# Normalized tokens of an attention phase written to DRAM by pairs of tiles, with the first pair's writes placed behind the third tile's loads

## The chip, the cores and the metric

One core of a Trainium2 chip runs the whole program. The metric is device time in microseconds (us), the median over several executions. The engines: PE is TensorE (matrix products), DVE is VectorE, ACT is ScalarE, POOL is GpSimd, and SP is SyncE, which computes nothing here and issues every DMA, one after the other, in program order. Each engine works through its own instruction list in order; an instruction that waits on a semaphore holds all that stand behind it on that engine.

## What is computed

One step of a one-layer hybrid encoder for 2048 prompt tokens and 32 sample tokens, D = 1024:

```python
n = rmsnorm(x, g_mix); z = n @ w_in            # q, k, v | GLA q, k, v | gate r | low-rank c
a = sink_attend(q, k, v, sinks, window of 128) # softmax per head, chunks of 64
g = rmsnorm(gla_chunked(qg, kg, vg, log_a)) * silu(r)
h = x + concat(a, g) @ w_out
y = h + relu(rmsnorm(h) @ w_up)**2 @ w_down
```

Outputs are y for prompt and sample tokens, the last 128 rows of k and v, and the GLA state. All is float32; a product is made of three passes of high and low parts (h and l).

## The kernel before

Tokens are worked on in 16 tiles of 128 (0 to 15) and one sample tile of 32 (named nt). There are three phases: attention, gated linear attention (GLA), feed-forward. The change lies in the attention phase and in the place where the GLA phase reads back what attention wrote.

**Per tile in the attention phase.** `front(t)` loads the transposed tokens `xT1a` (L249), scales them on DVE (L267), rounds them to a high part `nT..h` on ACT (L270) and takes the low part `nT..l` on POOL (L271). One pair of buffers (h and l) holds two tiles, an even one and the odd one after it; the pool of such buffers has 4, that is 2 pairs. `scales(t)` loads the tokens again untransposed as `x1a` (L244) and makes the row scale `rstd` by a square on ACT (L189) and a small iteration on DVE. `store(t)` writes three things to DRAM for the GLA phase: `rs` (L285: 128 rows of 4 bytes, one per partition), and the tile's halves of `nTh` and `nTl` (L287: 512 KB each). Then come the projections `zq`, `zkv`, `zr` on PE (all at L111), and `attend(t)`: transposes `qTp` and `kTp`, the copies `qT` (DVE, L456), `caT` (DVE, L395) and `kW` (ACT, L466), the scores `S`, a softmax (DVE L499 and L500, ACT L505), transposes `pT` and products `O`. The gate goes to DRAM as `rgd` (L375).

**The order.** The loop at L555 works on the front of the next tile while PE is at the current one. Tiles 0 and 1 are projected together first; the third tile, tile 2, is loaded in the loop's second step. `tc.issue_after(x)` keeps the DMAs in its block behind instruction x on SP. Otherwise a list scheduler with a timeline of its own sets each engine's order when the kernel is built. Weight loads go through five `io` buffers (`stage`, `x1a`, `xT1a`, `rg` and others share them), so a load waits until its buffer has been read.

**DMA semaphores.** SP's DMAs use eight semaphores in turn (DMAHW0 to DMAHW7). A DMA waits until the one eight places before it has landed.

**Reading back.** `gla_tokens(h, tiles)` (L620) loads the tokens of a pair of tiles into a buffer `nTb` (L627, one DMA per tile and part) and each tile's row scale, broadcast, into `rb` (L628).

Of the kernel before, what the change touches and what calls it, by code (L numbers as in the profile page):

```python
# [9 lines left out]
F32 = mybir.dt.float32  # L10
# [9 lines left out]
P = 128  # L20
D = 1024
KB = D // P
NT = 16
NS = 32
# [4 lines left out]
class Builder:  # L29
    def __init__(self, ctx, tc, a, o, nt=NT, ffn=True):  # L30
        self.ctx, self.tc, self.nc, self.a, self.o = ctx, tc, tc.nc, a, o
        self.nt, self.with_ffn = nt, ffn
        nc = self.nc
        self.V, self.S, self.G, self.T, self.Q = nc.vector, nc.scalar, nc.gpsimd, nc.tensor, nc.sync
        pool = lambda name, bufs, **kw: ctx.enter_context(tc.tile_pool(name=name, bufs=bufs, **kw))
        self.const = pool("const", 1)
        self.small = pool("small", 3)
        self.io = pool("io", 5)
        self.w = pool("w", 8)
        self.dram = pool("dram", 1, space=DRAM)  # L40
        self.psm = pool("psm", 3, space=PSUM)
        self.pss = pool("pss", 5, space=PSUM)
        tiles = list(range(nt)) + [nt]
        dt = lambda shape, name: self.dram.tile(shape, F32, tag=name, name=name)
        self.mixT = [dt([P, KB, self.rows(t)], f"mixT{t}") for t in tiles]
        self.nTd = [[dt([P, KB, self.rows(t)], f"nT{x}{t}") for x in "hl"] for t in tiles]
        self.cad = [dt([16, self.rows(t)], f"ca{t}") for t in tiles]
        self.rsd = [dt([self.rows(t), 1], f"rs{t}") for t in tiles]
        self.rgd = [dt([self.rows(t), 512], f"rgd{t}") for t in tiles]

        self.last_pe = self.last_table = None
        self.clock = 0.0
        self.state_clock = -1e9
        self.tasks = []
        self.seq = 0
# [174 lines left out]
    def attention_phase(self):  # L230
        tc, a, V, S, G, Q = self.tc, self.a, self.V, self.S, self.G, self.Q
        nt = self.nt
        w_in = a["w_in"].rearrange("(k p) n -> p k n", p=P)
        with ExitStack() as ctx:
# [4 lines left out]
            nT, st = {}, {}  # L239

            def load_x(t):
                r = self.rows(t)
                x = self.io_tile(f"x1a_{t}")[:r]
                Q.dma_start(x, self.x_src(t))  # L244
                return x

            def load_xT(t):
# [4 lines left out]
            def front(t, xT=None):  # L252

                r = self.rows(t)
                xT = xT or load_xT(t)
                if t == nt:
                    nT[t] = (*(c.tile([P, KB, NS], F32R, tag=f"nTs{x}", name=f"nTs{x}") for x in "hl"), 0)
                elif t % 2 == 0:
                    nT[t] = (*self.tok_pair(f"nT_{t}", 2 * P), 0)
                else:  # L260
                    nT[t] = (*nT[t - 1][:2], P)
                h, l, off = nT[t]
                ts = slice(off, off + r)
                step = 2 if t == 0 else 4
                for k in range(0, KB, step):
                    ks = slice(k, k + step)
                    V.tensor_tensor(  # L267
                        out=xT[:, ks], in0=xT[:, ks], in1=self.gmix[:, ks].unsqueeze(2).broadcast_to([P, step, r]), op=ALU.mult
                    )
                    S.activation(h[:, ks, ts], xT[:, ks], AF.Copy)  # L270
                    (V if t in (0, nt) else G).tensor_tensor(  # L271
                        out=l[:, ks, ts], in0=xT[:, ks], in1=h[:, ks, ts].bitcast(F32), op=ALU.subtract
                    )

            def scales(t, x=None):

                r = self.rows(t)
                x = x or load_x(t)
                V.tensor_copy(self.rstd[:r, t : t + 1], self.rms(x, x, r, f"a{t}"))

            def store(t):

                r = self.rows(t)
                h, l, off = nT[t]
                Q.dma_start(self.rsd[t], self.rstd[:r, t : t + 1])  # L285
                for x, dst in zip((h, l), self.nTd[t]):
                    Q.dma_start(dst, x[:, :, off : off + r].bitcast(F32))  # L287

            order = [*range(10), nt, *range(10, nt)]
            eng = (("act", "pool"), ("dve", "dve"))  # L290
# [35 lines left out]
            def project_q(t):  # L326
                r = self.rows(t)
                rs = self.rstd[:r, t : t + 1]
                qk = wk.tile([P, 5, 2, 64], F32, tag="qk", name=f"qk_{t}", bufs=3)
                sq = self.io_tile(f"sq_{t}")[:, :640].rearrange("p (j v d) -> p j v d", j=5, v=2)  # L330
                ps = self.ps_m(f"zq_{t}")[:r]
                token_gemm(ps, t, wq)
                pv = ps.rearrange("p (v j d) -> p j v d", v=2, j=4)
                S.activation(qk[:r, 0:4], pv, AF.Copy, scale=rs)
                S.activation(sq[:r, 0:4], pv, AF.Square, scale=rs)
                return qk, sq
# [31 lines left out]
            def project_gate(t):  # L368

                r = self.rows(t)  # L370
                rg = self.io_tile(f"rg_{t}")[:r, :512]
                ps = self.ps_m(f"zr_{t}")[:r]
                token_gemm(ps, t, wr)
                V.tensor_scalar(out=rg, in0=ps, scalar1=self.rstd[:r, t : t + 1], scalar2=None, op0=ALU.mult)
                Q.dma_start(self.rgd[t], rg)  # L375
# [180 lines left out]
            for i, t in enumerate(order):  # L556
                for j in order[i + 1 : i + 2 + (nt in order[i + 1 : i + 2])]:
                    if j not in nT:
                        front(j)
                        scales(j)  # L560
                        store(j)
                if i == 0:
                    z = {j: project_q(j) for j in order[:2]}
                    z = {j: project_kv(j, *z[j]) for j in z}
                    with tc.issue_after(self.weights_in):
                        store(t)
                        store(order[1])
                elif i > 1:
                    z[t] = project_kv(t, *project_q(t))
                if t == nt - 1:  # L570
                    self.prepare_gla(0)
                self.spawn(attend_sample(*z.pop(t)) if t == nt else attend(t, *z.pop(t)))
                if t != nt - 2:
                    project_gate(t)
                if t == nt - 1:
                    project_gate(t - 1)
                if t == nt:
                    self.load_gla_consts()
# [39 lines left out]
            self.wvg += self.wide_pairs(w_in, 1280, "wvg", self.GLA_ENG, (1,))  # L618

    def gla_tokens(self, h, tiles):  # L620
        pair = self.tok_pair(f"nTb_{h}", 288)
        rb = self.mid.tile([P, 288], F32, tag="rb", name=f"rb_{h}")
        off = 0
        for t in tiles:
            r = self.rows(t)
            for x, src in zip(pair, self.nTd[t]):
                self.Q.dma_start(x[:, :, off : off + r].bitcast(F32), src)  # L627
            self.Q.dma_start(rb[:, off : off + r], self.rsd[t].rearrange("r o -> o r").broadcast_to([P, r]))  # L628
            off += r
        return pair, off, rb  # L630
# [811 lines left out]
```

## Time and profile before

| | us |
|---|---|
| runs (median of 3, lowest, highest) | 2326.0, 2319.54, 2327.71 |
| the profiled execution | 2323.38 |
| its span, first to last instruction | 2321.6 |
| mean granted clock of TensorE | 0.979 of full speed |

Some 1.8 us of the profiled execution lie outside its span. PE is busy 97% of the span, DVE 61%, POOL 52%, ACT 41%. In the profile, "[7.28 <-ACT nT_2h L270]" behind an instruction says that its engine sat idle for 7.28 us before it and that this ACT instruction ended the wait. Numbers of buffers are left out there, so `nT_2h` stands for the buffer of tiles 2 and 3, and a name without its tile number can be that of any tile.

### The profile page before, as it was taken

How to read it: one execution, taken by the hardware profiler on the slowest of the kernel's cores; microseconds unless marked ns; L12 is line 12 of the kernel's file. 1: busy time of each engine (PE TensorE's matmuls, PEld its weight loads, DVE VectorE, ACT ScalarE, POOL GpSimd, SP SyncE). 2: the span in 40 equal slices, each digit the busy share in tenths (PEclk: the TensorE clock that was granted, in tenths of full speed). 3: DMA queues.
4: the chain of work that ended last, by engine and by line, in shares of the span. 5: the costliest groups of instructions: out<-in, count | busy, mean ns of one | idle time of the engine just before them, and what ended most of it. 6: DMA issues, size and time to landing. Idle time of an engine off the chain costs nothing.

```text
span 2321.6 us, 39805 instructions
## 1 busy us (share of the span) xinstructions
PE 2256.5 (97%) x15389; PEld 2117.4 (91%) x15389; DVE 1410.5 (61%) x3631; ACT 952.7 (41%) x1953; POOL 1197.3 (52%) x995
## 2 busy tenths in 40 slices
PE   6999998899998999999999999999999999999999
PEld 5777776788877999999999999999999999999999
DVE  6666656788888755555553755555554755555555
ACT  3554445455552643333434533333334533333331
POOL 3222224223241387667765566666655386666662
PEclk8999999889999999999999999999999999999999
DMA  8864564232322422222236222222227122222221
GB/s 204 159 130 109 122 149 154 56 95 70 103 84 76 129 76 91 92 74 73 73 103 181 75 81 73 73 73 73 73 63 218 55 73 73 73 73 73 73 64 52
DMA packets 214462, 221.57 MB, mean 95 GB/s; under 512 B 38736, under 2 KB 178976, under 8 KB 214272
## 3 DMA queue, kind: packets, MB, share of 16 engines
q1 hardware_dynamic: 214272, 219.02, 34.0%
q8 instruction: 121, 1.98, 0.4%
q14 instruction: 69, 0.57, 0.1%
HBM read 180.08 MB, written 38.91 MB: 94 GB/s over the span
## 4 chain that ended last, share of the span: by engine, by line
PE 75%; DVE 11%; DMA 5%; POOL 3%; ACT 3%; issue 2%; SPq 1%; DVEq 0%; POOLq 0%; ACTq 0%
PE dn L111 31%; PE PA22T L111 4%; PE PS3T L111 4%; PE PS2T L111 4%; PE PS4B L111 4%; PE PS1T L111 4%; PE PA11B L111 4%; PE PA12B L111 4%; PE zq L111 3%; PE op L111 3%; PE zr L111 3%; DVE AT L889 2%; PE zkv L111 2%; PE zv L111 2%; PE O L111 1%
## 5 line engine op out<-in xcount | busy, mean ns | idle before, releaser
L1100 POOL TENSOR_TENSOR wu<-stage,wu 128x512 fp32r<-128x512 f32 x336 | 432.2, 1297 | 469.2 <-ACT wu L1099 456.0
L1276 DVE TENSOR_TENSOR y<-y,dn 128x360 f32<-128x360 f32 (+1 forms) x768 | 393.1, 515 | 226.9 <-PE dn L111 224.2
L1099 ACT ACTIVATE wu<-stage 128x512 fp32r<-128x512 f32 x336 | 206.1, 628 | 493.7 <-PE dn L111 212.2
L1102 POOL TENSOR_TENSOR stage<-stage 128x512 f32<-128x512 f32 x192 | 249.3, 1298 | 7.5
L1229 ACT ACTIVATE r<-PA11B 128x360 f32<-128x360 f32 (+1 forms) x48 | 22.0, 459 | 283.6 <-PE PA11B L111 283.6
L1214 DVE TENSOR_TENSOR PA12B<-PA12B,r 128x360 f32<-128x360 f32 (+1 forms) x48 | 25.3, 527 | 150.6 <-PE PA12B L111 150.6
L716 POOL TENSOR_TENSOR g<-g,ggla 128x512 f32<-128x512 f32 (+1 forms) x17 | 25.2, 1501 | 170.0 <-ACT g L119 170.0
L111 PE MATMUL PA22T<-T4h,wu 128*128 128x360 f32 (+1 forms) x384 | 101.7, 328 | 0.0
L111 PE MATMUL PS2T<-T2h,wu 128*128 128x360 f32 (+1 forms) x384 | 99.4, 321 | 1.0 <-POOL wu L1100 0.6
L111 PE MATMUL PS3T<-T3h,wu 128*128 128x360 f32 (+1 forms) x384 | 100.2, 324 | 0.1
L111 PE MATMUL PS4B<-B22h,wu 128*128 128x360 f32 (+1 forms) x384 | 99.1, 321 | 0.0
L111 PE MATMUL PS1T<-T1h,wu 128*128 128x360 f32 (+1 forms) x384 | 98.9, 321 | 0.0
L111 PE MATMUL PA11B<-B11h,wu 128*128 128x360 f32 (+1 forms) x384 | 98.8, 321 | 0.0
L111 PE MATMUL PA12B<-B21h,wu 128*128 128x360 f32 (+1 forms) x384 | 98.7, 321 | 0.0
L889 DVE COPY_PREDICATED AT<-masks,A 64x64 f32<-64x64 int32 (+1 forms) x330 | 83.0, 253 | 13.8 <-PE A L111 3.9
L813 POOL TENSOR_TENSOR E<-cc 128x256 f32<-128x256 f32 (+1 forms) x117 | 68.3, 617 | 24.9 <-PE A L111 19.7
L505 ACT ACTIVATE P<-S,negm 128x192 f32<-128x192 f32 (+2 forms) x128 | 51.6, 418 | 53.0 <-DVE negm L500 36.1
L111 PEld LDWEIGHTS PA22T<-T4h,wu 128*128 128x128 f32 x384 | 70.3, 194 | 0.0
L111 PEld LDWEIGHTS PS2T<-T2h,wu 128*128 128x128 f32 x384 | 68.1, 188 | 1.8 <-ACT T2h L1132 1.0
L111 PEld LDWEIGHTS PS3T<-T3h,wu 128*128 128x128 f32 x384 | 69.2, 191 | 0.4 <-ACT T3h L1132 0.4
L111 PEld LDWEIGHTS PS1T<-T1h,wu 128*128 128x128 f32 x384 | 68.1, 188 | 0.0
L111 PEld LDWEIGHTS PS4B<-B22h,wu 128*128 128x128 f32 x384 | 68.1, 188 | 0.0
(1008 smaller groups left out, 7738.8 us busy)
## 6 DMA issues: line engine op xcount, KB each, us to landing
stage<-in_w_up SPq DMA_DIRECT2D x96, 512.0 KB, 3.8
stage<-in_w_down SPq DMA_DIRECT2D x96, 512.0 KB, 3.8
stage<-in_w_out SPq DMA_DIRECT2D x24, 512.0 KB, 4.2
xT1a<-in_xT_prompt SPq DMA_DIRECT2D x16, 512.0 KB, 6.8
stage<-in_w_in SPq DMA_DIRECT2D x16, 512.0 KB, 8.8
x1a<-in_x_prompt SPq DMA_DIRECT2D x16, 512.0 KB, 5.3
out_yT_prompt<-y SPq DMA_DIRECT2D x32, 180.0 KB, 5.2
m<-mixT SPq DMA_DIRECT2D x11, 512.0 KB, 4.1
```

What stands on the lines that cost most here:

```text
L111: self._pe(self.T.matmul(out, lhsT, rhs, start=start, stop=stop), ns)
L505: S.activation(Pt[:, u, :n], sp[:, jp], AF.Exp, bias=negm[:, ch, u : u + 1], scale=0.125, accum_out=rsum[:, ch, u : u + 1],)
L716: G.tensor_tensor(out=gv, in0=gv, in1=ggla[:r].unsqueeze(1).broadcast_to([r, 4, P]), op=ALU.mult)
L813: G.tensor_tensor(out=e4, in0=c4, in1=ref, op=ALU.subtract)
L889: V.copy_predicated(dst, mk.unsqueeze(1).broadcast_to([L // nh, 2, w // m, m]), src[r].rearrange("s p (n m) -> s p n m", m=m),)
L1099: self.after(S.activation(h, src, AF.Copy), after)
L1100: G.tensor_tensor(out=l, in0=src, in1=f32(h), op=ALU.subtract)
L1102: tt = lambda o, x, y, op: G.tensor_tensor(out=o, in0=x, in1=y, op=op)
L1214: tt = lambda out, x, y, op=ALU.add: V.tensor_tensor(out=out, in0=x, in1=y, op=op)
L1229: S.activation(r0, product(b, "A11", "B11"), AF.Copy)
L1276: V.tensor_tensor(out=yg[:, f, :], in0=yg[:, f, :], in1=ps, op=ALU.add)
```

## The change

Three edits. The DRAM buffers `nTd` hold a pair of tiles instead of one. `store(t)` writes `rs` for each tile as before, and `nTh` and `nTl` of both tiles of a pair in one DMA each after the odd tile (the sample tile on its own); `gla_tokens` reads them in the same size, and its buffer is as wide as its tiles need, so that a partition's row of a pair lies in one piece of 8 KB. And the stores of tiles 0 and 1 move from the loop's first step, behind the last weight load, to its second step, behind the load of tile 2's `x1a`.

```diff
-        self.nTd = [[dt([P, KB, self.rows(t)], f"nT{x}{t}") for x in "hl"] for t in tiles]
+        self.nTd = [[dt([P, KB, 2 * P if t < nt else NS], f"nT{x}{t}") for x in "hl"] for t in range(0, nt + 1, 2)]
...
-                Q.dma_start(x, self.x_src(t))
+                self.x_load = Q.dma_start(x, self.x_src(t)).ins
...
-                h, l, off = nT[t]
                 Q.dma_start(self.rsd[t], self.rstd[:r, t : t + 1])
-                for x, dst in zip((h, l), self.nTd[t]):
-                    Q.dma_start(dst, x[:, :, off : off + r].bitcast(F32))
+                if t == nt or t % 2:
+                    for x, dst in zip(nT[t], self.nTd[t // 2]):
+                        Q.dma_start(dst, x.bitcast(F32))
...
+                if i == 1:
+                    with tc.issue_after(self.x_load):
+                        store(0)
+                        store(1)
                 if i == 0:
                     z = {j: project_q(j) for j in order[:2]}
                     z = {j: project_kv(j, *z[j]) for j in z}
-                    with tc.issue_after(self.weights_in):
-                        store(t)
-                        store(order[1])
...
-        pair = self.tok_pair(f"nTb_{h}", 288)
+        pair = self.tok_pair(f"nTb_{h}", sum(self.rows(t) for t in tiles))
...
-            for x, src in zip(pair, self.nTd[t]):
-                self.Q.dma_start(x[:, :, off : off + r].bitcast(F32), src)
+            if t == nt or t % 2 == 0:
+                for x, src in zip(pair, self.nTd[t // 2]):
+                    self.Q.dma_start(x[:, :, off : off + src.shape[2]].bitcast(F32), src)
```

SP's list goes from 594 rows to 562. Line numbers of the changed kernel are one to four higher. The order of PE's instructions is the same in both kernels.

SP, early in the attention phase. Before, the six stores of tiles 0 and 1 (rs, nTh, nTl, twice) stand ahead of the small loads; these are the last rows of them and what follows, up to the load of tile 2's xT1a (`ck` to `masks` are small constants):

```order
L287 DMA nTl_93<-nT_0l 1024x1x128 [waits DMAHW7_49]
L285 DMA rs_144<-rstd 128x1 [waits DMAHW0_49,DVE_49]
L287 DMA nTh_94<-nT_0h 1024x1x128 [waits DMAHW1_49]
L287 DMA nTl_95<-nT_0l 1024x1x128 [waits DMAHW2_49]
L403 DMA ck<-in_cache_k 128x128 [waits DMAHW3_49]
L404 DMA cv<-in_cache_v 128x128 [waits DMAHW4_49]
L602 DMA wal<-in_w_alpha 16x256 [waits DMAHW5_49]
L603 DMA d_2829<-in_resets 128x288 [waits DMAHW6_49]
L604 DMA masks<-in_masks 128x224 [waits DMAHW7_49]
L628 DMA rb_4297<-rs_143 128x128 [waits DMAHW0_49]
L628 DMA rb_4297<-rs_144 128x128 [waits DMAHW1_49]
L249 DMA xT1a_528<-in_xT_prompt 128x1024 [waits DMAHW2_49,DVE_49]
```

The same place on SP in the changed kernel, from tile 2's xT1a (506) to tile 3's (587):

```order
L250 DMA xT1a_506<-in_xT_prompt 128x1024 [waits DMAHW2_49,DVE_49]
L245 DMA x1a_516<-in_x_prompt 128x1024 [waits DMAHW3_49,Pool_49]
L376 DMA rgd_144<-rg_478 128x512 [waits DMAHW4_49,DVE_49]
L285 DMA rs_127<-rstd 128x1 [waits DMAHW5_49]
L285 DMA rs_128<-rstd 128x1 [waits DMAHW6_49]
L288 DMA nTh_92<-nT_0h 128x2048 [waits DMAHW7_49]
L288 DMA nTl_93<-nT_0l 128x2048 [waits DMAHW0_49]
L632 DMA rb_4265<-rs_127 128x128 [waits DMAHW5_49,DMAHW1_49]
L632 DMA rb_4265<-rs_128 128x128 [waits DMAHW6_49,DMAHW2_49]
L250 DMA xT1a_587<-in_xT_prompt 128x1024 [waits DMAHW3_49,Activation_49]
```

Tile 2's load now stands ahead of the stores. The two `rs` stores follow each other, and the two `rb` loads, which wait for them (DMAHW5 and DMAHW6 are theirs), stand ahead of tile 3's load.

ACT at the same place, before, from the rounding of tile 2 (`nT_2h<-xT1a_528`) to the first exponentials; `xT1a_607` is tile 3's, `kW_600` and `kW_675` are the key windows of tiles 0 and 1:

```order
L270 ACTIVATE nT_2h<-xT1a_528 128x4x128 [waits DMAHW2_49,DVE_49]
L270 ACTIVATE nT_2h<-xT1a_528 128x4x128 [waits DVE_49]
L189 ACTIVATE x1a_538,ss_a_540<-x1a_538 128x1024 [waits DMAHW3_49,Pool_49]
L466 ACTIVATE kW_600<-kTp_588 128x128 [waits DVE_49]
L270 ACTIVATE nT_2h<-xT1a_607 128x4x128 [waits DMAHW6_49,DVE_49]
L270 ACTIVATE nT_2h<-xT1a_607 128x4x128 [waits DVE_49]
L466 ACTIVATE kW_675<-kTp_663 128x128 [waits DVE_49]
L505 ACTIVATE P_0_681,rsum_679<-S_0_0_682,negm_678 128x64 [waits DVE_49,PE_49]
```

And in the changed kernel, from the key window of tile 0 (`kW_580`) to that of tile 1 (`kW_655`); `xT1a_587` is tile 3's:

```order
L467 ACTIVATE kW_580<-kTp_568 128x128 [waits DVE_49]
L506 ACTIVATE P_0_661,rsum_659<-S_0_0_662,negm_658 128x64 [waits DVE_49,PE_49]
L506 ACTIVATE P_0_661,rsum_659<-S_0_0_662,negm_658 128x64
L506 ACTIVATE P_0_661,rsum_659<-S_0_1_663,negm_658 128x64 [waits DVE_49,PE_49]
L506 ACTIVATE P_0_661,rsum_659<-S_0_1_663,negm_658 128x64
L382 ACTIVATE es_0_676<-es_0_676 128x4 [waits DVE_49]
L335 ACTIVATE qk_617<-zq_619,rstd 128x512 [waits PE_49]
L336 ACTIVATE sq_618<-zq_619,rstd 128x512 [waits Activation_49]
L271 ACTIVATE nT_2h<-xT1a_587 128x4x128 [waits DMAHW3_49,DVE_49]
L271 ACTIVATE nT_2h<-xT1a_587 128x4x128 [waits DVE_49]
L467 ACTIVATE kW_655<-kTp_643 128x128 [waits DVE_49]
```

In both, the key window of tile 1 stands behind the rounding of tile 3; that rounding has moved behind tile 0's exponentials and tile 2's `qk` and `sq`.

PE, in the changed kernel, where it first needs tile 1's key window, in the middle of tile 2's projections (in the kernel before the rows are the same, with `kW_675`):

```order
L112 MATMUL zkv_691<-wkvh,nT_2h 128x272
L112 MATMUL zkv_691<-wkvl,nT_2h 128x272
L112 MATMUL zkv_691<-wkvh,nT_2l 128x272
L112 MATMUL S_0_0_742<-kW_655,qT_649 128x192 [waits Activation_49,Pool_49]
L112 MATMUL S_0_1_743<-kW_655,qT_649 128x192 [waits DVE_49]
L112 MATMUL S_0_0_742<-kW_655,qT_649 128x192
L112 MATMUL S_0_1_743<-kW_655,qT_649 128x192
```

Nothing has moved on PE; the first S row of tile 1 waits for ACT's `kW_655`.

## Rows read from the trace of the kernel before

**Rows 1.** Who waited longest on PE, whole program: total us, times, longest us.
```profile
PE zq L111 <- ACT nT_2h L270: 7.3, 1, 7.3
...
PE O L111 <- ACT pS L535: 3.5, 2, 3.1
```

**Rows 2.** Three stretches: us, then busy us (and instructions) of PE, its weight loads, DVE, ACT, POOL, then TensorE's granted clock, busy share of the DMA engines, GB/s.
```profile
47.90:55.10 7.20, 0.00 (x0) 0.00 (x0) 1.40 (x3) 0.67 (x2) 0.00 (x0) 0.64 0.86 272
55.10:60.38 5.28, 5.08 (x11) 3.55 (x12) 3.04 (x14) 1.76 (x4) 2.75 (x3) 0.52 0.62 150
60.38:340.00 279.62, 279.45 (x1618) 215.94 (x1617) 182.50 (x703) 142.35 (x464) 70.62 (x118) 1.00 0.63 136
```

**Rows 3.** The chain that ended last, in order of time: start us, us, what.
```profile
31.65 17.41 DMA nTl<-nT_0l
...
49.13 4.54 DMA xT1a<-in_xT_prompt
...
54.43 1.24 ACT nT_2h L270 x2
...
71.89 9.91 DMA xT1a<-in_xT_prompt
...
125.10 2.75 PE zq L111 x12
```

**Rows 4.** PE in order of time: start us, us, instruction. The first row is the last product of tile 1, the second the first of tile 2; twelve products of tile 2 lie from there to the third row; the fourth is tile 1's S.
```profile
47.43 0.40 PE L111 MATMUL zr<-wr1h,nT_0l 128*128 128x512 f32 x1
55.11 0.80 PE L111 MATMUL zq<-wq0h,nT_2h 128*128 128x512 f32 x1 [7.28 <-ACT nT_2h L270]
...
60.61 0.40 PE L111 MATMUL zq<-wq1h,nT_2h 128*128 128x512 f32 x1
...
68.80 0.92 PE L111 MATMUL S<-kW,qT 64*128 64x192 f32 x8
```

**Rows 5.** SP in order of time: start us, us of the issue itself, DMA.
```profile
26.72 0.43 SPq L315 DMA_DIRECT2D gk<-in_g_k  x1
...
31.65 5.84 SPq L287 DMA_DIRECT2D nTl<-nT_0l  x1
...
45.37 0.43 SPq L604 DMA_DIRECT2D masks<-in_masks  x1
47.06 1.25 SPq L628 DMA_DIRECT2D rb<-rs  x2
49.13 0.33 SPq L249 DMA_DIRECT2D xT1a<-in_xT_prompt  x1
```

**Rows 6.** DVE in order of time: the last low part of the weights, tile 0's gate, tile 1's keys, then tile 2's scaling.
```profile
34.67 1.22 DVE L206 TENSOR_TENSOR wr1l<-stage,wr1h 128x1024 fp32r<-128x1024 f32 x1
...
41.80 0.75 DVE L374 TENSOR_SCALAR rg<-zr,rstd 128x512 f32<-128x512 f32 x1 [0.69 <-PE zr L111]
...
43.32 0.29 DVE L357 TENSOR_TENSOR kn<-qk,gk 128x128 f32<-128x128 f32 x1
53.70 1.29 DVE L267 TENSOR_TENSOR xT1a<-xT1a,packed 128x512 f32<-128x512 f32 x2 [10.09 <-DMA xT1a<-in_xT_prompt]
```

**Rows 7.** The stores of rs (line L285), whole program, with the time from issue to landing.
```profile
L285 SPq DMA_DIRECT2D rs<-rstd x17: 318/367/1220, 27.2 to 335.8; - x17
...
DMA to landing us min/median/max: 7.3/9.0/17.9
```

**Rows 8.** Stretches around stores of rs, columns as in rows 2.
```profile
28.00:31.00 3.00, 3.00 (x14) 3.00 (x15) 2.89 (x7) 2.63 (x4) 0.65 (x1) 0.50 1.23 267
31.00:37.00 6.00, 6.00 (x39) 5.85 (x39) 4.91 (x10) 1.77 (x7) 4.08 (x5) 0.84 0.92 26
37.00:40.00 3.00, 3.00 (x15) 2.48 (x14) 3.00 (x21) 0.18 (x1) 0.94 (x4) 1.00 2.02 295
40.00:47.00 7.00, 7.00 (x36) 5.84 (x35) 2.85 (x8) 0.00 (x0) 0.00 (x0) 1.00 0.65 25
...
322.00:338.00 16.00, 16.00 (x97) 12.38 (x96) 10.05 (x36) 8.96 (x31) 5.29 (x9) 1.00 1.03 291
339.00:348.00 9.00, 9.00 (x62) 7.76 (x61) 2.96 (x11) 2.14 (x4) 0.00 (x0) 1.00 0.89 45
```

**Rows 9.** SP at the sample tile's rs store (32 rows of 4 bytes): its issue, and that of the first `rb` load, which waits for it to land.
```profile
209.95 0.32 SPq L285 DMA_DIRECT2D rs<-rstd  x1
...
213.42 0.82 SPq L628 DMA_DIRECT2D rb<-rs  x2
```

**Rows 10.** The tile of xT1a from 20 to 75 us: ns min/median/max, first and last start.
```profile
L267 DVE TENSOR_TENSOR xT1a<-xT1a,packed x4: 684/688/693, 53.7 to 62.2; 128x512 f32<-128x512 f32 x4
L270 ACT ACTIVATE nT_2h<-xT1a x4: 629/630/631, 54.4 to 62.9; 128x512 fp32r<-128x512 f32 x4
```

**Rows 11.** SP and PE at the end of the attention phase, in order of time.
```profile
335.81 0.74 SPq L285 DMA_DIRECT2D rs<-rstd  x1
336.64 1.00 SPq L549 DMA_DIRECT2D mixT<-aT  x1
337.70 3.01 SPq L200 DMA_DIRECT2D stage<-in_w_in  x4
```

More of the change, by code (lines that the diff above doesn't have):

```diff
@@ L620, in gla_tokens @@
     def gla_tokens(self, h, tiles):
-        pair = self.tok_pair(f"nTb_{h}", 288)
+        nt = self.nt
+        pair = self.tok_pair(f"nTb_{h}", sum(self.rows(t) for t in tiles))
         rb = self.mid.tile([P, 288], F32, tag="rb", name=f"rb_{h}")
```

## The prediction

> **What bounds the kernel now.** I read the table of engines first, then who waited longest on PE, then the chain of waits, then PE, SP and DVE in order of time over the first 75 us, and last the DMA rates by stretch. The table of engines has PE busy for 97% of the span, so only a wait on PE, or a stretch in which PE runs at the lower clock, is worth anything. The list of PE's waits has at its head the place at which the change aims: 7.3 us in one piece, for the rounded tokens of tile 2 [rows 1]. In the stretch of this wait PE does nothing, in the next 5.28 us its granted clock is 0.52, the 1.2 GHz level, and from there to 340 us PE is busy for 279.45 of 279.62 us at full clock [rows 2]. So what is gained or lost at that place moves everything behind it by as much, as long as nothing else in the attention phase becomes late.
>
> The chain of waits tells why: a store of nT_0l takes 17.41 us, then the load of tile 2 is issued at 49.13, lands after 4.54, and DVE, ACT and PE follow [rows 3]. SP shows the queue: the issue of that store alone holds SP for 5.84 us, the constants behind it are through at 45.8, and then the rb loads go ahead of the load [rows 5].
>
> Why the stores are slow is in the rates. After each store of rs there are 2 to 3 us at a usual rate, 267 and 295 GB/s, and then 6 and 7 us at 26 and 25 GB/s, though the DMA engines count as busy [rows 8]. The same follows the store issued at 335.81: 45 GB/s from 339 to 348 us [rows 8, 11]. The large stores, in 512-byte rows, move at 291 GB/s before it [rows 8]. It is the 128 rows of 4 bytes that clog the DMA engines, not the megabytes: such a store of 0.5 KB lands 9.0 us after its issue (median), 7.3 at the least [rows 7].
>
> **What the change removes.** With the six stores gone from ahead of it, SP goes from gk at 26.72 through the constants at some 0.45 us each, to tile 2's load. That load still waits for its buffer, which the last low part of the weights frees: 34.67 + 1.22 = 35.9 [rows 6]. Issued at 36.0, with nothing large in flight, and landing after the 4.54 us of rows 3, it is there at 40.5. DVE is busy with tile 1's keys until 43.6 [rows 6]; then come 0.69 on DVE and 0.63 on ACT [rows 10], so the first rounded tokens are there at 44.9, before PE is done with tile 1 (47.43 + 0.23 = 47.66) [rows 4]. The wait goes entirely. PE's twelve first products of tile 2 would end at 47.66 + 2.75 = 50.4, with 2.75 from the same twelve at full clock [rows 3], instead of at 60.61 [rows 4]. **Term 1: -10.2 us**, of which 7.45 are the wait and 2.75 the low clock.
>
> **What the change adds.** The stores are not gone; they now lie ahead of tile 3's load. On SP: rgd of tile 0 waits for its gate, 41.80 + 0.75 = 42.55 [rows 6], so the first rs store is issued at 43.0, the second at 43.4, then 2 MB of nTh and nTl. The two rb loads wait for the two rs stores to land, and tile 3's load stands behind them. Waiting behind it are DVE's scaling of tile 3 and, on DVE, the rest of tile 0's softmax; on ACT, the rounding of tile 3 and the key window of tile 1, which PE needs in the middle of tile 2's projections. PE gets there at 68.80 in the kernel before [rows 4], hence at 58.6 now.
>
> When do two rs stores in a row land? No stretch of the trace shows two. The first lands at 43.0 + 9.0 = 52.0 [rows 7]. The second adds nothing if they overlap, so it lands at 52.4; if they add up it costs at least the clogged part of one, 6 to 7 us, and at most the whole 9.0 [rows 7, 8]: 58 to 61. I take 7.0, thus 59.0, for the sample tile's row: its store of 32 rows had landed at most 3.47 us after its issue (209.95 to 213.42) [rows 9], against 9.0 for 128 rows, so the time goes with the number of rows, as it would if they were served one after another.
>
> Below 512 bytes the DMA engines read, modify and write, says the Trainium skill (DMA: Bandwidth & Descriptors, Specifications). If each engine does so for its rows in turn, a second store queues behind the first, and by that rule the sum is the one below; the rows alone, which hold no two such stores in a row, leave the overlap open. The page gives no price for one such row.
>
> With 59.0, the second rb load and then tile 3's load go out at 59.6. At 4.54 us, as when the load of tile 2 followed the same stores [rows 3], it lands at 64.1. Then DVE 0.69, ACT twice 0.63 [rows 10] and the key window, some 0.3 (an estimate, half of a rounding): 66.3. PE waits from 58.6: **term 2: +7.7 us**. A wait of 7.28 us brought the low clock once already [rows 2, 4], so **term 3: +2.75 us**, the price of term 1. The ends of term 2: 1.0 with overlap (load out at 52.9, landed 57.4, key window 59.6; ACT's own rows ahead of it end at about the same time), without term 3; and 15.1 with both rs stores at 9.0 and a load that takes 9.91, as the load of tile 4 did behind an rs store [rows 3]: out at 61.6, landed 71.5, key window 73.7.
>
> **The rest.** SP issues 32 DMAs fewer and the pairs move in longer rows; from 60.38 to 340 us PE loses 0.17 us in all [rows 2], so this is worth nothing there, and the cover is large: a load for a tile is out a whole tile ahead. At the end of the attention phase the GLA weights still go out right behind an rs store [rows 11], so the clog ahead of them stays, and with it the 3.1 us that PE waits there for ACT [rows 1]. Twice as many bytes of the last pair lie ahead of that store now, in longer rows; I take 0, between -3.1 (the wait goes) and +1.8 (512 KB more for each of h and l, at 291 GB/s in 2 x 1.8, half of it won back by the longer rows). The order of wvg's casts against the softmax moves too; PE's only waits there are parts of the same 3.5 us [rows 1], so 0. In the feed-forward phase nothing moves.
>
> **Sum.** -10.2 + 7.7 + 2.75 = +0.25 us, made against the profiled execution's 2323.4: 2323.6. That execution lies 2.6 us under the median of the runs, within their spread of 8.2. A measurement of this kernel can tell about 0.5% from no change, that is 11.6 us.
>
> **Rivals.**
> *The two rs stores overlap.* Then term 2 is 1.0 and term 3 is 0: -9.2, that is 2314.2 us. For it: the two go to different places in DRAM, and 2 to 3 us of other traffic pass behind an rs store at a usual rate [rows 8], so an engine does not simply stop at it. Against it: 32 rows against 128 [rows 9, 7].
> *Slower: tile 3's load is caught in the clog itself.* It takes 9.91 instead of 4.54 and both stores 9.0 [rows 3, 7]: 15.1 + 2.75 - 10.2 = +7.7, that is 2331.1 us. It decides from a landing at 63.9 on: later than that, the wait with its low clock costs more than the 10.2 gained. For it: 2 MB and the rb loads are queued ahead. Against it: rb waits for the landing of both rs stores, so the clog is over when the load goes out, and what is left of 2 MB passes at 291 GB/s.
> *The load of tile 2 is not earlier.* If its buffer came free only with a later reader, the wait at 55.11 would stay: 2323.4. Against it: before, DVE had nothing to do from 43.6 to 53.7 [rows 6], so every reader of that buffer was long done.
>
> **How the numbers follow.** Forecast (both stores add up) 0.58, overlap 0.27, slower 0.11, not earlier 0.04. The predicted time is the forecast's, 2323.6. The range reaches below the overlap case by the 3.1 us at the end of the attention phase, 2311, and above to 2330, short of the far end of the slower rival. The forecast's own range, with the second store at 6.0 to 9.0, is 2322.6 to 2325.6. Faster by over 0.5% means under 2314.4: two thirds of the overlap case, 0.18. Slower by over 0.5% would be above 2337.6, beyond all cases worked out: 0.03. The remaining 0.79 is within 0.5%.
>
> **What would show it.** Right: PE goes from tile 1's last gate product to tile 2 without a wait at 47.7, and tile 2's load is issued at about 36; then one PE wait of about 8 us at some 58.6, before tile 1's S, ended by ACT's kW, with the granted clock at half behind it; tile 3's load issued near 59.6; the DMA rate at 25 to 60 GB/s from 46 to 59. The overlap case shows as a load issued near 53 and a wait of about 1 us. Term 1 is wrong if PE still waits for nT_2h near 48; term 2 is wrong if tile 3's load goes out before the second rs store has landed; the rest is wrong if PE's waits between 75 and 340 us come to more than 2 us, or if PE's wait for ACT at the end of the attention phase goes.

## Result and the profile after

The changed kernel takes 2329.94 us (median of 20 runs, 2324.78 to 2333.74), the kernel before 2324.32 us in the same comparison (20 runs, 2317.91 to 2328.2): ratio 1.002, 95% interval 1.0013 to 1.0028, by that ratio some 4.7 us slower. The profiled execution took 2327.38 us, its span is 2325.6; the forecast was 2323.6.

PE's waits between 44 and 130 us in the changed kernel (who was waited for: total us, times, longest):

```profile
PE pT L116 <- DVE qT L457: 5.7, 1, 5.7
PE S L112 <- ACT kW L467: 4.8, 1, 4.8
```

The wait for nT_2h at the head of [rows 1] is gone; two others, 10.6 us together, stand in its place. PE in order of time (start, us, instruction) at the places of [rows 4] and three further on: tile 2's first and thirteenth product, tile 1's S, tile 3's first product, a pT with the wait for qT, and the next S:

```profile
47.64 0.39 PE L112 MATMUL zq<-wq0h,nT_2h 128*128 128x512 f32 x1
50.36 0.39 PE L112 MATMUL zq<-wq1h,nT_2h 128*128 128x512 f32 x1
...
63.43 1.65 PE L112 MATMUL S<-kW,qT 64*128 64x192 f32 x8 [4.84 <-ACT kW L467]
...
73.97 0.39 PE L112 MATMUL zq<-wq0h,nT_2h 128*128 128x512 f32 x1
...
86.89 0.69 PE L116 MATMUL pT<-packed,Pb 128*128 128x128 f32 x2 [5.73 <-DVE qT L457]
...
90.85 0.92 PE L112 MATMUL S<-kW,qT 64*128 64x192 f32 x8
```

In the kernel before the first three stand at 55.11, 60.61 and 68.80 [rows 4], and the other three here:

```profile
76.48 0.39 PE L111 MATMUL zq<-wq0h,nT_2h 128*128 128x512 f32 x1
...
83.83 0.44 PE L115 MATMUL pT<-packed,Pb 128*128 128x128 f32 x2 [0.17 <-DVE qT L456]
...
86.28 0.92 PE L111 MATMUL S<-kW,qT 64*128 64x192 f32 x8
```

So PE is ahead by 7.47, then 10.25, then 5.37, then 2.51, and then behind by 3.06 and 4.57 us. Behind that it stays so: a product of zr at 357.27 before stands at 361.13 after (+3.86), and the spans end 4.0 apart. Nearly all of it is decided between 47 and 91 us. Why, SP shows (issue, us of the issue itself, DMA):

```profile
34.80 0.33 SPq L250 DMA_DIRECT2D xT1a<-in_xT_prompt  x1
...
42.95 0.92 SPq L285 DMA_DIRECT2D rs<-rstd  x2
43.91 0.43 SPq L288 DMA_DIRECT2D nTh<-nT_0h  x1
44.39 0.43 SPq L288 DMA_DIRECT2D nTl<-nT_0l  x1
50.32 2.08 SPq L632 DMA_DIRECT2D rb<-rs  x2
52.50 0.38 SPq L250 DMA_DIRECT2D xT1a<-in_xT_prompt  x1
...
55.09 0.32 SPq L285 DMA_DIRECT2D rs<-rstd  x1
...
73.46 0.32 SPq L285 DMA_DIRECT2D rs<-rstd  x1
73.87 0.38 SPq L250 DMA_DIRECT2D xT1a<-in_xT_prompt  x1
```

Tile 2's load goes out at 34.80. Tile 3's goes out at 52.50, behind the rb loads as foreseen, and tile 4's at 73.87, right behind tile 3's rs store. The first two rs stores, with the time from issue to landing:

```profile
L285 SPq DMA_DIRECT2D rs<-rstd x2: 423/435/447, 42.9 to 43.4; - x2
...
DMA to landing us min/median/max: 7.3/8.0/8.6
```

The first landed at 50.3 and the second at 52.0, and the two rb loads went out with them. When the loads of tiles 3 and 4 landed, DVE's scaling shows (in brackets the idle time before it and what ended it):

```profile
61.16 1.29 DVE L268 TENSOR_TENSOR xT1a<-xT1a,packed 128x512 f32<-128x512 f32 x2 [7.12 <-DMA xT1a<-in_xT_prompt]
...
84.88 1.29 DVE L268 TENSOR_TENSOR xT1a<-xT1a,packed 128x512 f32<-128x512 f32 x2 [7.57 <-DMA xT1a<-in_xT_prompt]
```

Tile 3's load took 8.6 us, tile 4's 11.0. What lay ahead of them, the stretches tell (columns as in [rows 2]):

```profile
42.90:46.00 3.10, 3.10 (x15) 2.59 (x14) 1.87 (x4) 1.77 (x3) 1.00 (x1) 1.00 1.46 254
46.00:52.50 6.50, 6.50 (x37) 5.25 (x36) 3.61 (x17) 0.78 (x3) 1.82 (x3) 1.00 0.71 25
52.50:56.50 4.00, 4.00 (x33) 3.52 (x34) 1.46 (x6) 2.54 (x11) 0.00 (x0) 1.00 0.87 344
...
65.00:69.00 4.00, 4.00 (x11) 2.81 (x9) 2.71 (x14) 4.00 (x18) 1.84 (x4) 0.50 0.99 268
...
76.00:84.80 8.80, 5.16 (x33) 3.56 (x30) 1.31 (x4) 1.08 (x3) 0.00 (x0) 0.92 0.58 85
```

As in [rows 8], an rs store is followed by 3 us at a usual rate and then by some 6.5 us at 25 GB/s. Here the two stand side by side and clog once; only behind that does what is left of the pair's 2 MB pass, at 344 GB/s, and tile 3's load with it. At 65 PE runs at the 1.2 GHz level behind its wait.

### The profile page after: what moved, and what is told of

It reads as the page before. It is cut to its first block, busy times and chain, and to the rows that moved or that the text cites. A ratio compares the mean times of both kernels' runs of the same rounds, so it can differ in the third digit from the quotient of the medians.

```text
span 2325.6 us, 39745 instructions
## 1 busy us (share of the span) xinstructions
PE 2253.9 (97%) x15389; PEld 2115.5 (91%) x15389; DVE 1411.2 (61%) x3631; ACT 952.7 (41%) x1953; POOL 1198.8 (52%) x995
## 4 chain that ended last, share of the span: by engine, by line
PE 74%; DVE 11%; POOL 4%; DMA 4%; issue 4%; ACT 2%; SPq 1%; POOLq 0%; DVEq 0%; ACTq 0%
PE dn L112 29%; PE PS4B L112 4%; PE zq L112 4%; PE zr L112 4%; PE PA22T L112 4%; PE PS3T L112 4%; PE PS2T L112 4%; PE PS1T L112 4%; PE PA11B L112 4%; PE PA12B L112 4%; PE op L112 3%; DVE AT L893 2%; PE zkv L112 2%; PE zv L112 2%; PE O L112 1%
```

## The experiments

The question was which of three things makes the loads late: the place of the first pair's stores, SP's wait ahead of the rb loads, or the rs stores themselves. The first kernels move things, the later ones take the rs stores' form away. Together (issue: SP; scaled: DVE's first instruction on it; idle and clock: PE from 44 to 130 us; last wait: PE's longest wait for pS, at the end of the phase; ratio: to the kernel before in the same comparison):

| kernel | tile 3 issued, scaled | tile 4 issued, scaled | PE idle | clock | last wait | us | ratio to before (95%) |
|---|---|---|---|---|---|---|---|
| before | 56.26, 61.55 | 71.89, 81.82 | 7.6 | 0.94 | 3.1 | 2324 to 2327 | 1 |
| changed | 52.50, 61.16 | 73.87, 84.88 | 10.6 | 0.92 | 3.4 | 2329.9 | 1.002 (1.0013 to 1.0028) |
| e1 pairing alone | 45.00, 53.24 | 60.70, 77.09 | 5.4 | 0.98 | 3.0 | 2321.6 | 0.9987 (0.9977 to 0.9997) |
| e2 move alone | 62.94, 68.85 | 82.13, 93.48 | 20.5 | 0.88 | 3.0 | 2334.1 | 1.0042 (1.003 to 1.0055) |
| e3 rb late | 44.03, 57.66 | 69.47, 77.72 | 5.6 | 0.94 | 4.4 | 2326.6 | 1.0012 (1.0001 to 1.0022) |
| e4 stores behind tile 3 | 43.42, 50.55 | 72.36, 84.05 | 12.0 | 0.92 | 3.0 | 2329.6 | 1.0021 (1.0012 to 1.003) |
| e5 rs behind loads | 52.01, 60.00 | 65.43, 75.11 | 4.8 | 0.98 | 9.8 | 2328.6 | 1.0008 (0.9997 to 1.0019) |
| e6 one rs, moved | 42.71, 52.70 | 58.65, 69.02 | 0 | 1.00 | 0 | 2305.2 | 0.9906 (0.9891 to 0.9922) |
| e7 one rs, kernel before | 46.22, 51.34 | 55.94, 70.26 | 0 | 1.00 | 0.5 | 2308.0 | 0.9918 (0.9903 to 0.9934) |
| e8 one rs, pairs at old place | 42.19, 49.33 | 54.13, 68.50 | 0 | 1.00 | 0.2 | 2308.7 | 0.9917 (0.99 to 0.9933) |
| e10 rs in 256-byte rows | 45.97, 54.69 | 66.72, 70.52 | 0.5 | 1.00 | 0.4 | 2308.5 | 0.992 (0.9905 to 0.9935) |

### e1 and e2: each half of the change alone

e1 keeps the changed kernel's pairs and puts the first pair's stores back:

```diff
-                if i == 1:
-                    with tc.issue_after(self.x_load):
-                        store(0)
-                        store(1)
 ...
+                    with tc.issue_after(self.weights_in):
+                        store(t)
+                        store(order[1])
```

> The pairing alone: the first pair's stores stand at their old place, ahead of tile 2's load, but as two rs stores and then two stores of a whole pair. Theory (what costs time is the rs stores and what is queued behind them, and two rs stores that are issued next to each other clog the DMA engines only once): both land by about 36, the 2 MB of the pair follow by about 43, tile 2's load goes out at about 36 and lands at 43 to 45, PE's wait for nT_2h of 7.3 us shrinks to 0 to 2 us, and no wait of more than 2 us takes its place at tiles 3 and 4: 2313 to 2318 us beside 2324 for the kernel before. Rival (the pairing is worth nothing, as I predicted for everything behind the first pair): the wait of some 7 us for nT_2h stays, 2322 to 2326 us.

The wait at tile 2 shrinks as the theory said, to 1.7 us for nT_2h and 0.7 for nT_2l, but the kernel gains only 0.13%: 2321.6 us where 2313 to 2318 were expected. Two more numbers failed. Tile 2's load went out at 43.62, not 36: SP held it for the landing of a store it had issued earlier (who SP waited for between 30 and 50 us):

```profile
SPq L250 <- DMA nTl<-nT_0l: 3.5, 1, 3.5
SPq L631 <- DMA nTh<-nT_0h: 2.5, 1, 2.5
```

Tile 4's load, right behind tile 3's rs store at 60.28, took 16 us although it was issued 11 us earlier than before; PE waited 3.0 us for qT. The wait at the end of the phase stayed, too.

e2 takes the kernel before and moves the first pair's single-tile stores behind tile 2's load:

```diff
+                if i == 1:
+                    with tc.issue_after(self.x_load):
+                        store(0)
+                        store(1)
 ...
-                    with tc.issue_after(self.weights_in):
-                        store(t)
-                        store(order[1])
```

> The move alone: the first pair's stores by single tiles as before (rs, nTh, nTl of tile 0, then of tile 1), issued behind tile 2's load. Theory (a load that is queued behind rs stores is late, wherever they stand): no wait for nT_2h, but tile 3's load lands at 63 to 67, later than in the changed kernel (61.2) because the two rs stores do not stand side by side, so PE waits 6 to 10 us for kW before tile 1's S and again at tile 4: 2326 to 2333 us. Rival (the whole pairs, in rows of 8192 bytes, hold the load of tile 3 up): no wait for kW over 1 us, 2313 to 2317 us.

It came out worse than the theory's upper end: PE waits 13.3 us for kW and 7.2 us for qT. The two rs stores have 1 MB between them (42.16 and 44.03), and clog twice (stretches, columns as before):

```profile
46.00:53.00 7.00, 7.00 (x41) 5.69 (x40) 4.80 (x21) 0.28 (x1) 1.04 (x2) 1.00 0.90 21
53.00:56.00 3.00, 3.00 (x25) 2.61 (x23) 0.60 (x4) 2.54 (x11) 0.61 (x1) 1.00 1.35 301
56.00:62.50 6.50, 1.83 (x16) 1.55 (x12) 0.00 (x0) 0.00 (x0) 0.00 (x0) 0.96 0.97 30
```

So the pairing helps, by making one clog of two (in e1 there is one, 27 GB/s from 31 to 38 us, in the kernel before there are two [rows 8]), and the move harms.

### e3, e4 and e5: moving what stands ahead of a load

e3 issues the rb loads behind the last tile's loads:

```diff
-            self.Q.dma_start(rb[:, off : off + r], self.rsd[t].rearrange("r o -> o r").broadcast_to([P, r]))
+            with self.tc.issue_after(self.x_load):
+                self.Q.dma_start(rb[:, off : off + r], self.rsd[t].rearrange("r o -> o r").broadcast_to([P, r]))
```

> The changed kernel with the rb loads issued at the end of the attention phase, so that tile 3's load no longer stands behind a wait for the rs stores. It goes out near 45 instead of 52.5. Theory A (the DMA engines hold it: clog until 52, then 2 MB): it still lands only at 57 to 60, PE's wait for kW falls from 4.8 to 1 to 3 us, tile 4's load goes out earlier and its wait falls below 4 us: 2318 to 2324 us. Theory B (SP's wait ahead of the rb loads holds it, my prediction's mechanism): it lands at 50 to 53, no wait for kW, 2312 to 2316 us.

Tile 3's load went out 8.5 us earlier than in the changed kernel and was there 3.5 us earlier, after 13.6 us in the DMA engines: theory A, at the places it named (2.2 us for kW, 3.4 for qT). As a whole it stayed above A's range.

e4 issues the first pair's stores one tile later, at `i == 2` instead of `i == 1`:

```diff
-                if i == 1:
+                if i == 2:
                     with tc.issue_after(self.x_load):
```

> The changed kernel with the first pair's stores issued behind the loads of tile 3 instead of tile 2. Theory (each wait comes from a load that stands behind rs stores): tile 3's load lands by 53, no wait for kW near 58.6; three rs stores stand side by side near 51; tile 4's load still stands behind tile 3's rs store and lands some 10 us after its issue; if it goes out by 64 the wait for qT is below 2 us and the time is 2313 to 2317 us. Rival (the wait only moves on to the next load): PE waits 5 us or more at tile 4, 2319 to 2325 us.

The rival: the wait for kW is gone and tile 4 has one of 11.9 us. The time, 2329.6, lies above the rival's range as well. Tile 4's load is next on SP behind the rs store at 63.04 and went out at 72.36. SP's longest wait for a DMA from 30 to 95 us:

```profile
SPq L250 <- DMA nTl<-nT_0l: 9.0, 1, 9.0
```

Between nTl and this load SP issues rs, nTh, ca, two rb, nTl and rs. The load is the eighth behind nTl; in e1, too, it was the eighth (ck, cv, wal, resets, masks, two rb lie between), and there too the load waited for nTl.

e5 issues each rs store from tile 2 on behind the loads of the tile after it:

```diff
 ...
                         front(j)
                         scales(j)
+                        if late:
+                            with tc.issue_after(self.x_load):
+                                store_rs(late.pop())
+                        late.append(j)
                         store(j)
 ...
```

> The changed kernel with the rs store of each tile from tile 2 on issued behind the loads of the tile after it, so that tile 4's load no longer stands right behind tile 3's rs store. Nothing else is moved. Theory (PE's second wait, 5.7 us for qT at 86.9, comes from the rs store ahead of tile 4's load, which is late itself because DVE was held at tile 3): tile 4's load goes out near 67, behind nTl of the second pair, and lands by 74; the wait for qT and the low clock behind it go, the wait for kW of 4.8 us stays: 2319 to 2323 us. Rival (tile 4's load is late for another reason, the 2 MB of the second pair): the wait for qT stays over 4 us, 2326 to 2330 us.

At tile 4 as the theory said: no wait for qT, kW as it was. But not the time. At the end of the phase PE waits 9.8 us. It was 5.0 us ahead of the kernel before in front of that wait and 1.86 behind after it:

```profile
353.23 1.12 PE L112 MATMUL O<-pS,v 128*64 128x256 f32 x4 [9.80 <-ACT pS L537]
```

```profile
351.63 1.06 ACT L203 ACTIVATE wqgh<-stage 128x1024 fp32r<-128x1024 f32 x1 [13.16 <-DMA stage<-in_w_in]
```

ACT stands at the cast of the first GLA weights, whose loads were issued at 334.01, behind an rs store at 332.37. The profiled execution is the fastest of the twelve (2322.56), so the trace does not show what the median of 2328.6 adds to that. In each of these kernels a load that stands behind an rs store pays for it.

### e6, e7 and e8: one store of rstd

PE turns the 17 columns of rstd into rows at the end of the phase, and one DMA stores them; the same is computed. e6 is the changed kernel with this, e7 the kernel before, e8 is e1:

```diff
 ...
-                Q.dma_start(self.rsd[t], self.rstd[:r, t : t + 1])
 ...
+            pp = self.ps_s("rsT")[: nt + 1, :P]
+            self.tr(pp, self.rstd)
+            rsT = c.tile([nt + 1, P], F32, tag="rsT", name="rsT")
+            S.activation(rsT, pp, AF.Copy)
+            Q.dma_start(self.rsd, rsT)
 ...
-            ... self.rsd[t].rearrange("r o -> o r").broadcast_to([P, r])
+            ... self.rsd[t : t + 1, :r].broadcast_to([P, r])
```

> The changed kernel without its 17 rs stores of 4-byte rows: at the end of the attention phase PE turns the 17 columns of rstd into 17 rows (one transposition of 128x17, one copy on ACT), and one DMA stores them in rows of 512 bytes, from which the rb loads read. The same outputs are computed. Theory (the rs stores, not the megabytes, make every one of these waits): tile 3's load goes out near 45 and lands by 54, tile 4's right behind the second pair; no wait over 1 us at tiles 2, 3 and 4, and the 3.4 us for pS at the end shrink: 2309 to 2314 us. Rival (the 2 MB of a pair, in rows of 8192 bytes, hold the loads behind them): a wait for kW of 2 us or more stays, 2315 to 2322 us.

> The kernel before, its stores by single tiles at their old place, with the same single store of rstd in place of the 17 rs stores. Theory (the rs stores make the wait at tile 2 that the change was aimed at): tile 2's load goes out near 37 in spite of the 2 MB ahead of it and lands by 43, PE's 7.3 us for nT_2h go: 2310 to 2315 us, as with the stores moved. Rival (the 2 MB in rows of 512 bytes hold the load): a wait for nT_2h of 3 us or more stays, 2317 to 2324 us.

> The pairing at the old place, with the single store of rstd: the first pair goes out as two DMAs ahead of tile 2's load. Theory: without rs stores it matters neither where the first pair's stores stand nor how long their rows are: tile 2's load goes out at about 36, no wait over 1 us at tiles 2 to 4, 2309 to 2314 us, within 2 us of the other two kernels with one store of rstd. Rival: one of the three places or row lengths still shows a wait of 3 us or more, and its time is 4 us or more above the best.

All three gain some 0.8 to 0.9%, more than expected, and their intervals overlap: without rs stores it is not measurable whether the change is there, nor whether the rows of nT have 512 bytes (e7, 0.9918) or 8 KB (e8, 0.9917). PE from 44 to 130 us, in the kernel before, the changed kernel and e6 (columns as before), one line each:

```profile
44.00:130.00 86.00, 78.36 (x441) 60.67 (x441) 52.54 (x201) 41.26 (x132) 22.29 (x34) 0.94 0.79 159
```

```profile
44.00:130.00 86.00, 75.42 (x417) 59.64 (x416) 50.51 (x191) 39.07 (x128) 21.82 (x33) 0.92 0.69 147
```

```profile
44.00:130.00 86.00, 86.00 (x505) 68.54 (x504) 60.84 (x233) 45.17 (x154) 24.58 (x40) 1.00 0.44 154
```

In e6 PE is never idle there and always at full clock; the same bytes of nT lie ahead of the same loads. e6 is the fastest by median, 0.94% under the kernel before (0.78 to 1.09).

### e9: what makes the rs store dear

e6 with 14 further stores that nobody reads, at the old place of the rs stores; `width` and `pitch` are words in DRAM:

```diff
 ...
+            width, pitch = ((1, 1), (1, P), (16, 16), (16, P), (64, 64), (64, P), (P, P))[t % 7]
+            self.probe[t] = (dt([P, pitch], f"pr{width}p{pitch}t{t}"), width)
 ...
+                    Q.dma_start(dst[:, :width], rstw[:, :width])
 ...
```

> The kernel with one store of rstd, stores moved, and in addition one store per tile from tile 2 to 15 that nobody reads, issued when the tile's rstd is there, at the rs store's old place: 128 rows each, in seven forms that follow one another, each form twice. Rows of 4, 64 and 256 bytes, each once lying end to end in DRAM and once 512 bytes apart, and rows of 512 bytes. It measures what makes the rs store dear. Theory A (a row under 512 bytes is read, modified and written, so each costs alike): all forms under 512 bytes land 7 to 9 us after their issue and leave the DMA engines at 25 to 60 GB/s for some 6 us, end to end or apart; rows of 512 bytes land within 3.5 us. Theory B (rows that share a stretch of 512 bytes in DRAM wait for one another): rows 512 bytes apart land within 3.5 us whatever their width, rows of 4 bytes end to end in 7 to 9 us, 64 bytes end to end in between. Theory C (the 128 rows as such): all seven forms land in 7 to 9 us. As a whole the run lies between the kernel with one store (2305 us) and the changed kernel (2330 us).

The run took 2303.6 us (a single one), no more than e6. Landing by form (count, KB each, median us; the names give width and pitch, 1 is 4 bytes, 128 is 512):

```profile
pr128p128t<-rstw SPq DMA_DIRECT2D x2, 64.0 KB, 4.1
...
pr64p64t<-rstw SPq DMA_DIRECT2D x2, 32.0 KB, 2.0
pr64p128t<-rstw SPq DMA_DIRECT2D x2, 32.0 KB, 2.7
...
pr16p16t<-rstw SPq DMA_DIRECT2D x2, 8.0 KB, 4.4
pr16p128t<-rstw SPq DMA_DIRECT2D x2, 8.0 KB, 1.4
pr1p1t<-rstw SPq DMA_DIRECT2D x2, 0.5 KB, 9.8
pr1p128t<-rstw SPq DMA_DIRECT2D x2, 0.5 KB, 5.2
```

The two of a form can differ with what else is under way, and for some forms only one landing is on record. 4-byte rows end to end landed after 11.8 us (issued at 139.05 among 401 GB/s) and 7.9 us (at 299.84, few other transfers); 512 bytes apart after 1.4 us (at 158.10, no other transfers) and 8.9 us (at 321.94, among 397 GB/s). In a quiet stretch, then, 128 rows of 4 bytes cost 7.9 us in one 512-byte stretch and 1.4 in 128 of them. Rows of 256 bytes landed after 1.6 us end to end (at 242.47) and 1.4 apart (at 262.14). Each of these is one store. Among other traffic the two 4-byte forms differ in what follows them (stretches, columns as before):

```profile
142.00:150.00 8.00, 8.00 (x46) 6.47 (x45) 6.12 (x29) 4.39 (x21) 2.49 (x6) 1.00 1.16 115
...
325.00:333.00 8.00, 8.00 (x46) 6.97 (x46) 6.82 (x27) 4.45 (x16) 2.48 (x6) 1.00 1.04 380
```

Behind the rows end to end the load of 512 KB issued at 140.37 took 10.9 us; behind the rows 512 bytes apart the other transfers kept 380 GB/s. Theory B, for the ends of the scale; the 64 bytes end to end had other traffic (405 GB/s) and stay open, and with them how near to each other rows must lie to be dear.

### e10: the clog and SP's wait held apart

e6 took away the 4-byte rows and the rb loads' early wait at once. e10 is the changed kernel with the same DMAs in the same order; only each rs store has rows of 256 bytes:

```diff
 ...
+                V.tensor_copy(rsw[t % 3][:r, :1], self.rstd[:r, t : t + 1])
 ...
-                Q.dma_start(self.rsd[t], self.rstd[:r, t : t + 1])
+                Q.dma_start(self.rsd[t].rearrange("o (r c) -> (o r) c", c=64), rsw[t % 3][:r])
 ...
```

> The changed kernel with every DMA at its place and the rb loads still waiting for the rs stores; only each rs store writes 128 rows of 256 bytes, end to end, instead of 128 rows of 4 bytes (rstd in the first word of each row, ones in the rest, one small copy on DVE per tile more). The rb loads read the first 128 words, so that the values of rb, and with them the outputs of the GLA phase, are not those of the reference; durations do not depend on them. It holds apart the two things that e6 took away together: the clog and the wait of the rb loads. Theory (the clog alone made the later waits): both rs stores have landed by 47, rb is issued at about 47, tile 3's load by 48, landing by 55, no wait for kW over 1 us and none for qT over 1 us at tile 4: 2306 to 2312 us. Rival (SP's wait ahead of the rb loads and the 2 MB of the pair are enough): a wait for kW of 2 us or more stays, 2315 us or more.

The theory; rb and tile 3's load went out even earlier than it said. SP, then the stretch that was at 25 GB/s in the changed kernel:

```profile
41.73 0.91 SPq L289 DMA_DIRECT2D rs<-rsw  x2
42.69 0.45 SPq L292 DMA_DIRECT2D nTh<-nT_0h  x1
43.18 0.43 SPq L292 DMA_DIRECT2D nTl<-nT_0l  x1
43.71 2.17 SPq L636 DMA_DIRECT2D rb<-rs  x2
45.97 1.21 SPq L253 DMA_DIRECT2D xT1a<-in_xT_prompt  x1
```

```profile
46.00:52.50 6.50, 6.50 (x38) 5.25 (x37) 4.61 (x21) 0.28 (x1) 0.61 (x2) 1.00 0.70 229
```

The two rs stores landed 1.8 and 1.6 us after their issue, both by 43.8 instead of 52.0. Tile 3's load follows the rb loads as in the changed kernel and takes 8.7 us (8.6 there); but it goes out 6.5 us earlier, and PE is idle for 0.5 us from 44 to 130 us. Without the 4-byte rows the same order of DMAs costs next to nothing. The other values of rb do not show in the durations: between 400 and 1000 us the 1664 products A<-E took 231 ns each in the mean, 233 in e8.

## Why the prediction was wrong, by its own steps

**What bounds the kernel** was read right: 128 rows of 4 bytes clog the DMA engines, not the megabytes [rows 7, 8]. e6, e7, e8 and e10 show it.

**Term 1 (-10.2) held**: 10.25 us ahead at tile 2's thirteenth product, tile 2's load out at 34.80, no wait.

**Term 2 (+7.7) came out as +4.84, for another reason.** The step that two rs stores add up failed: issued side by side they had landed by 50.3 and 52.0, not 52.0 and 59.0. The second cost some 1.7 us more, not 7.0, so that tile 3's load went out at 52.50 instead of 59.6, close to the overlap rival's 52.9. e2 shows that they add up when 1 MB of other stores lies between them, as in the kernel before [rows 8]. That rival's price of 1.0 was wrong too, and so was the step behind both: that a load issued once rs has landed takes 4.54 us. It took 8.6, because what was left of the pair's 2 MB had stood behind the clog and was still to come; in e10 and e6, with no clog ahead, a load behind the same 2 MB took 8.7 and 8.1. I had the point in hand ("what is left of 2 MB passes at 291 GB/s"), as an argument against the slower rival, and gave it no microseconds. Out 7.1 us earlier than forecast and 4.1 us longer under way, the load left the term 2.9 us too large.

**Term 3 (+2.75) held** once there was a wait of 4.84 us: from 5.37 ahead to 2.51 is 2.86.

**"The rest: nothing" is the step that turned a gain into a loss.** The text named its own refutation, more than 2 us of waits between 75 and 340 us; at one place there are 5.73, and with the low clock behind them PE goes from 2.51 ahead to 4.57 behind: 7.08 us. "A load for a tile is out a whole tile ahead" was not so at tile 4. Before, its load was issued at 71.89 behind tile 3's rs store, took 9.91 us and lay on the chain that ended last [rows 3], and PE got at 83.83 to the qT that DVE copies behind that tile's scaling, and waited 0.17. That wait was so short only because PE came so late. What PE won at tile 2 it could not have kept beyond this place unless tile 4's load came earlier as well, and it came later. The rs store ahead of it waits for tile 3's rstd. In the chain that ended last, tile 3's x1a load, from which that rstd is made, takes 11.05 us:

```profile
53.87 11.05 DMA x1a<-in_x_prompt
```

From 66.19 to 73.37 the chain then runs over DVE, which makes rstd and works off softmax by turns; it had been held at tile 3 until 61.16. In the changed kernel's order the rstd stands behind the first step (mx) of the softmax of tile 1's second S, in the kernel before ahead of it. DVE in the changed kernel, then in the kernel before:

```profile
70.36 0.55 DVE L500 TENSOR_REDUCE mx<-S 128x2 f32<-128x384 f32 x1
...
73.28 0.15 DVE L280 COPY rstd<-rsq_y_a 128x1 f32<-128x1 f32 x1
```

```profile
71.29 0.15 DVE L279 COPY rstd<-rsq_y_a 128x1 f32<-128x1 f32 x1
...
73.96 0.55 DVE L499 TENSOR_REDUCE mx<-S 128x2 f32<-128x384 f32 x1
```

So tile 3's rs store came at 73.46 instead of 71.47, and the load behind the store with it. Ahead of the prediction stand the orders of SP, ACT and PE, not that of DVE. e5, where that load does not stand behind the store, has no wait there, and e3, e1 and e4 have 3.0 to 11.9.

With the measured sizes the terms are -10.25 + 4.84 + 2.86 + 7.08 = +4.5, against 4.57 at that place and 4.0 at the end of the profiled spans; without the last they are -2.55. That the forecast of +0.25 lies so near the 4.7 measured is luck: term 2 was 2.9 us too large, and the rest left out 7.1.

**Rows below 512 bytes.** The prediction drew on the Trainium skill (DMA: Bandwidth & Descriptors, Specifications): below 512 bytes the DMA engines read, modify and write. That rule alone names no difference between 4-byte and 256-byte rows. The measurement does: 7.9 against 1.6 us in quiet stretches, and 4-byte rows 512 bytes apart 1.4. What costs is not the short row as such but 128 of them in the same 512 bytes. That they wait for one another's read and write there would explain it; no run looked into the memory.

**Open.** The end of the phase and the GLA phase add their own differences: at the S that stands at 86.28 before, e1 was 3.6 us ahead (82.66) and measured 3.0 faster at the end (2324.64 to 2321.62); e3 was 2.1 ahead (84.19) and measured slower (1.0012). Stretches of low clock fall elsewhere from kernel to kernel there; I did not follow them.

## What to carry to other kernels

Before moving a slow transfer, ask what makes it slow and whether that can go: six kernels that move it, or what stands beside it, gave 0.9987 to 1.0042; changing its form gave 0.99. When a wait is removed, look along the same engine for the next place that was late by almost nothing (0.17 us here); the gain lasts only until there, unless what it waits for moves too. And give every row that you name as a risk its microseconds in the sum.

## What the hardware showed that I had not expected

128 rows of 4 bytes that lie in one 512-byte stretch of DRAM land after 7.3 us or more [rows 7], 7.9 in a quiet stretch, and leave other transfers at 21 to 30 GB/s for 6 to 7 us (45 for 9 us at the end of the phase [rows 8]); the same rows 512 bytes apart, in a quiet stretch, land after 1.4 us. Two such stores issued within 1 us clogged once (7.3 and 8.6 us to landing); with 1 MB between them, twice. In this program SP issues a DMA only when the one eight places ahead has landed, as the waits of e1 (3.5 us) and e4 (9.0 us) show, so that one store that lands late holds loads that have nothing to do with it.
